# Eight pairs of heads in one pipeline per layer, with a written order for TensorE and more work for GpSimd

## The chip, the cores and the metric

The kernel runs on one core of a Trainium2 chip. A core has five engines that each work through a queue of their own in order: TensorE (PE, the matrix engine; PEld is its weight load), VectorE (DVE), ScalarE (ACT), GpSimd (POOL) and SyncE (SP), which here issues most of the transfers. They meet only at semaphores. The metric is the time of one execution on the device in microseconds. The kernel before takes 591.89 us (median of 3 runs, 590.76 to 593.34).

## What is computed

A trunk of two decoder layers on 256 tokens of width 1024, in float32. Layer 0 has two groups of heads side by side, layer 1 one group of 16 heads; each layer is followed by a SwiGLU network.

```python
proj = h @ w_in                                   # layer 0: c_q 256, c_kv 128, k_r 32, then qB, kB, vB of 512 each
qA = (rmsnorm(c_q, g_q) @ w_uq)                   # 8 latent heads, 64 plain + 32 rotary columns
kv = (rmsnorm(c_kv, g_kv) @ w_ukv)                # k_nope 64 and vA 64 for each head
oA = causal_attention([q_nope, rope(q_rope)], [k_nope, rope(k_r)], vA)
oB = dilated_attention(qB, kB, vB)                # 8 heads of 64, a bias for each head
h = h + concat(oA, oB) @ w_out
...
qkv = h @ w_qkv                                   # layer 1: 16 query heads, 2 key/value heads
s = q @ k.T * scale - slopes * dist               # a band of 128 keys, one sink for each head
o = softmax([s, sink])[..., :-1] @ v
h = h + o @ w_out
...
h = h + (silu(gate) * up) @ w_down                # behind the attention of each layer
```

## The kernel before

**Products.** Each float32 operand is split in two fp32r halves: a rounded half (`hi`, a cast on ACT) and the rest (`lo`, a difference on DVE). `mm3` (L106 to L116) then makes one product of three matmuls: hi by hi, hi by the weights' lo, lo by hi. A "job" below is one such triple with 512 columns.

**Weights.** `load` (L55) brings 128x2048 pieces into `raw` (three buffers) from SP's queue; `part_weight` (L70) casts them to `wh` on ACT (L83) and forms their rest `wl` on DVE (L84), in blocks of 128x512 (416 and 352 for uq). A `raw` buffer is free for the next load once its last `wl` is formed.

**Stages.** On the time axis of the profile: the c projection (0 to 17 us); the projections b, uq and ukv with the norms of c and the rotary terms (17 to 45); four pairs of latent heads "a" (45 to 79); four pairs of dilated heads "b" (79 to 113); the end of the output projection wo0 (113 to 121); the first SwiGLU network (121 to 302); kv and the first half of qc (302 to 328); eight pairs of grouped heads "c" in two calls of four (328 to 392); the end of wo1 (392 to 402); the second network (402 to 577); the end.

**One pair of heads** (`Pair`, L349) goes through: `turns` (transposes T of q and k into the PSUM bank `t`, copied to SBUF by DVE and ACT); `scores` (s, into the banks `s0` and `s1`); `softmax` (sn on DVE L373, the exponential e on ACT L378, its reciprocal and the normalising of e on DVE L383, one instruction of 128 and one of 256 columns for each head); `turn_p` for each of the two heads (transposes pT into the bank `p`, split by ACT and DVE, L395); `values` (o, into the bank `t` again, split into `oT` by ACT and DVE in two halves, L409). Each of the banks `t`, `s0`, `s1`, `p` is there once.

**What sets the order.** `attention` (L440) writes the pairs one after another, with jobs of a projection as fill between the steps: the rest of b beside the latent pairs, kt 0 to 3 of wo0 beside the dilated ones, the second half of qc beside the grouped pairs 0 to 3, kt 0 to 3 of wo1 beside 4 to 7. A scheduler of the compiler then orders the instructions of every engine by its own estimate, so the order on TensorE is not the written one: it can use fill up earlier. `OutProj.finish` does kt 4 to 7 of the output projection after the last pair. GpSimd does little: constants, the power in the norms (L197), rotary terms (L251 to L256, and L314 to L319 for one half) and copies of the sinks (L370).

Of the kernel before, what the change touches and what calls it, by code (L numbers as in the profile page):

```python
# [11 lines left out]
F32 = mybir.dt.float32  # L12
# [4 lines left out]
P = 128  # L17
D = 1024
KT = D // P
# [21 lines left out]
def trunk(ctx: ExitStack, tc: tile.TileContext, dr):  # L41
# [13 lines left out]
    def load(name, parts=1, between=None):  # L55
# [12 lines left out]
        st["raw"].append((raw, width, cut, u))  # L68

    def part_weight(name, between=None):  # L70

        _, n, kts = dr[name]
        st = streams[name]
        raw, width, cut, u = st["raw"].pop(0)
        per = n * kts
        for i in range(width // per):
            hi = wpool.tile([P, 1024], F32R, tag="wh", name=f"wh_{name}_{u}_{i}")
            lo = wpool.tile([P, 1024], F32R, tag="wl", name=f"wl_{name}_{u}_{i}")
            step = min(per, cut, 512 if per == 1024 else 416)
            for a in range(0, per, step):  # L80
                e = min(per, a + step)
                part = raw[:, i * per + a : i * per + e]
# [180 lines left out]
    def project(wname, base, per, groups, out, scale, name, parted=()):  # L263

        jobs = []
        for j in groups:
            hold = {}

            def job(j, q, b, hold):
                if q == 0 and b == 0:  # L270
                    hold["p"] = [acc(f"{name}{j}{i}") for i in range(2)]
                for i in range(per):
                    kt = per * q + i
                    mm3(hold["p"][b], actT(b, kt), piece(wname, base(j) + q).at(i, 0, 512), kt == 0, kt == KT - 1)
                if q == KT // per - 1 and j in parted:
# [7 lines left out]
                elif q == KT // per - 1:  # L283
                    t = big.tile([P, 512], F32, tag="big", name=f"{name}s{j}{b}")
                    nc.scalar.activation(t, hold["p"][b], AF.Copy, scale=scale[b])
                    out[j][b] = t

            for q in range(KT // per):
                for b in range(2):
                    jobs.append(lambda j=j, q=q, b=b, hold=hold: job(j, q, b, hold))  # L290
# [4 lines left out]
    for f in bjobs[:12]:  # L295
        f()
# [52 lines left out]
    class Pair:  # L349
# [12 lines left out]
        def softmax(self, name, ps, bias, sink):  # L362
# [76 lines left out]

    def attention(pairs, kt0, fill):  # L440
        n = len(pairs)
        total = len(fill)

        def run(share):

            want = total - int(round(total * min(1.0, share)))
            while len(fill) > want:
                fill.pop(0)()

        step = 1.0 / (n + 1)  # L450
        pairs[0].turns()
        for i in range(n + 1):
            t = i * step
            if i < n:
                pairs[i].scores()
            run(t + step / 4)
            if i > 0:
                pairs[i - 1].turn_p(0)
                run(t + step / 2)
                pairs[i - 1].turn_p(1)  # L460
            if i + 1 < n:
                pairs[i + 1].turns()
            run(t + 3 * step / 4)
            if i > 0:
                pairs[i - 1].values(kt0 + i - 1)
            run(t + step)


    def latent(p):
        half, store = p // 2, {}  # L470

        def turns():
            for i in range(2):
                k = 2 * (p % 2) + i
                pt = transposes([t[half][:, k, :] for t in (qA[0], qA[1], kA[0], kA[1])], f"a{p}{i}", 96)
                qk = work.tile([P, 512], F32, tag="qk", bufs=3, name=f"qk_a{p}{i}")
                nc.vector.tensor_copy(qk[:96, 0:256], pt[:96, 0:256])
                nc.scalar.copy(qk[:96, 256:512], pt[:96, 256:512])
                store[i] = qk

# [12 lines left out]

    attention([latent(p) for p in range(4)], 0, bjobs[12:])

    biases = {}
# [8 lines left out]
    def pair64(p, name, q, k, zk, v, bias0, sinks):  # L505

        store = {}

        def turns():
            pt = transposes([*q(), *(k() if k else ())], f"{name}{p}")  # L510
# [6 lines left out]
        return Pair(  # L517
            f"{name}{p}", turns, pair_scores(lambda: store["q"], zk), v, lambda i: bias_of(bias0 + 2 * p + i), 0.125,
            [None if sinks is None else sinks[:, 2 * p + i : 2 * p + i + 1] for i in range(2)])

    class OutProj:
        def __init__(self, wname, name):
            self.w, self.name, self.po, self.done = wname, name, None, 0

        def one(self, kt, b):
            if self.po is None:
                self.po = [[acc(f"{self.name}{b}{n}") for n in range(2)] for b in range(2)]
            for n in range(2):
                self.mm(kt, b, n)

        def mm(self, kt, b, n):
            w = piece(self.w, kt).at(0, n * 512, n * 512 + 512)
            mm3(self.po[b][n], oact(b, kt), w, kt == 0, kt == 7)

        def jobs(self, kts):
            return [lambda kt=kt, b=b: self.one(kt, b) for kt in kts for b in range(2)]

        def finish(self, kts, g):
            for b in range(2):
                for n in range(2):  # L540
                    for kt in kts:
                        self.mm(kt, b, n)
                    new_h(b, self.po[b][n], n, g, self.name)

# [7 lines left out]

    attention([dilated(p) for p in range(4)], 4, out0.jobs(range(4)))

# [84 lines left out]
    g = gain(0)  # L639
    out0.finish(range(4, 8), g)  # L640
    g1 = gain(1)
# [42 lines left out]
    out1.finish(range(4, 8), g)  # L684

# [120 lines left out]
```

## Time and profile before

| what | value |
|---|---|
| median of 3 runs | 591.89 us (590.76 to 593.34) |
| the profiled execution | 591.09 us, of it 589.3 us span |
| TensorE busy | 566.9 us (96%) |
| VectorE busy | 381.1 us (65%) |
| ScalarE busy | 335.7 us (57%) |
| GpSimd busy | 26.4 us (4%), 63 instructions |
| granted TensorE clock, mean | 0.990 |

The span runs from the first to the last instruction; 1.8 us of the execution lie outside it. A matmul's record is longer than the distance to the next one, since they overlap in the pipeline; so a busy TensorE may still hold short gaps, and where distances matter they are taken from start to start.

### The profile page before, as it was taken

How to read it: one execution, taken by the hardware profiler on the slowest of the kernel's cores; microseconds unless marked ns; L12 is line 12 of the kernel's file. 1: busy time of each engine (PE TensorE's matmuls, PEld its weight loads, DVE VectorE, ACT ScalarE, POOL GpSimd, SP SyncE). 2: the span in 40 equal slices, each digit the busy share in tenths (PEclk: the TensorE clock that was granted, in tenths of full speed). 3: DMA queues.
4: the chain of work that ended last, by engine and by line, in shares of the span. 5: the costliest groups of instructions: out<-in, count | busy, mean ns of one | idle time of the engine just before them, and what ended most of it. 6: DMA issues, size and time to landing. Idle time of an engine off the chain costs nothing.

```text
span 589.3 us, 7570 instructions
## 1 busy us (share of the span) xinstructions
PE 566.9 (96%) x2661; PEld 458.6 (78%) x2661; DVE 381.1 (65%) x842; ACT 335.7 (57%) x732; POOL 26.4 (4%) x63
## 2 busy tenths in 40 slices
PE   8999996999999999999999999889999999999995
PEld 5788875778888888888888766658888888888884
DVE  5589987696556655554468787877556556654524
ACT  6789766575455555543447867756555455554412
POOL 1250000010000000100000010001000000000000
PEclk9999997999999999999999999999999999999998
DMA  8967442337564554645628353026555565555301
GB/s 254 379 232 251 143 162 89 107 108 253 176 214 152 205 185 172 213 155 204 212 73 297 132 180 123 39 71 211 204 194 182 175 214 155 204 191 174 136 2 71
DMA packets 18183, 101.57 MB, mean 172 GB/s; under 512 B 2272, under 2 KB 3168, under 8 KB 7520
## 3 DMA queue, kind: packets, MB, share of 16 engines
q1 hardware_dynamic: 17712, 100.55, 49.6%
q10 hardware_dynamic: 432, 0.53, 0.2%
q8 instruction: 21, 0.34, 0.2%
q14 instruction: 18, 0.15, 0.1%
HBM read 100.02 MB, written 1.05 MB: 172 GB/s over the span
## 4 chain that ended last, share of the span: by engine, by line
PE 86%; DVE 4%; ACT 4%; DMA 2%; issue 2%; SPq 1%; POOL 1%; POOLq 0%; ACTq 0%; DVEq 0%
PE f1g L114 7%; PE f0g L116 7%; PE f0g L114 7%; PE f1g L116 7%; PE f0g L115 7%; PE f1g L115 7%; PE f0d L116 3%; PE f0d L115 3%; PE f0d L114 3%; PE f1d L116 3%; PE f1d L114 3%; PE f1d L115 3%; PE p L114 2%; PE p L115 2%; PE p L116 2%
## 5 line engine op out<-in xcount | busy, mean ns | idle before, releaser
L84 DVE TENSOR_TENSOR wl_gu<-raw_gu,wh_gu 128x512 fp32r<-128x512 f32 x176 | 115.5, 688 | 63.8 <-ACT wh_gu L83 63.3
L83 ACT CAST wh_gu<-raw_gu 128x512 fp32r<-128x512 f32 x176 | 102.2, 619 | 79.4 <-PE f0g L116 33.1
L84 DVE TENSOR_TENSOR wl_dn<-raw_dn,wh_dn 128x512 fp32r<-128x512 f32 x88 | 57.5, 689 | 54.8 <-ACT wh_dn L83 54.8
L83 ACT CAST wh_dn<-raw_dn 128x512 fp32r<-128x512 f32 x88 | 50.8, 619 | 61.6 <-PE f1d L116 23.3
L114 PE MATMUL f1g<-wh_gu,hTh_p 128*128 128x512 f32 x176 | 69.7, 396 | 0.5 <-ACT hTh_p L131 0.5
L114 PE MATMUL f0g<-wh_gu,hTh_p 128*128 128x512 f32 x176 | 69.6, 395 | 0.0
L116 PE MATMUL f0g<-wh_gu,hTl_p 128*128 128x512 f32 x176 | 68.9, 392 | 0.0
L116 PE MATMUL f1g<-wh_gu,hTl_p 128*128 128x512 f32 x176 | 68.8, 391 | 0.0
L115 PE MATMUL f0g<-wl_gu,hTh_p 128*128 128x512 f32 x176 | 68.5, 389 | 0.0
L115 PE MATMUL f1g<-wl_gu,hTh_p 128*128 128x512 f32 x176 | 68.5, 389 | 0.0
L116 PEld LDWEIGHTS f0g<-wh_gu,hTl_p 128*128 128x128 f32 x176 | 33.0, 188 | 7.4 <-DVE hTl_p L132 0.5
L116 PEld LDWEIGHTS f1g<-wh_gu,hTl_p 128*128 128x128 f32 x176 | 33.0, 188 | 7.4 <-DVE hTl_p L132 0.4
L114 PEld LDWEIGHTS f1g<-wh_gu,hTh_p 128*128 128x128 f32 x176 | 33.1, 188 | 7.1 <-ACT hTh_p L131 0.8
L114 PEld LDWEIGHTS f0g<-wh_gu,hTh_p 128*128 128x128 f32 x176 | 33.1, 188 | 6.8 <-ACT hTh_p L131 0.4
L115 PEld LDWEIGHTS f0g<-wl_gu,hTh_p 128*128 128x128 f32 x176 | 33.1, 188 | 6.6
L115 PEld LDWEIGHTS f1g<-wl_gu,hTh_p 128*128 128x128 f32 x176 | 33.1, 188 | 6.5
L114 PE MATMUL f0d<-wh_dn,f0fTh 128*128 128x512 f32 x88 | 34.5, 392 | 0.0
L114 PE MATMUL f1d<-wh_dn,f1fTh 128*128 128x512 f32 x88 | 34.3, 390 | 0.0
L116 PE MATMUL f0d<-wh_dn,f0fTl 128*128 128x512 f32 x88 | 34.3, 390 | 0.0
L116 PE MATMUL f1d<-wh_dn,f1fTl 128*128 128x512 f32 x88 | 34.2, 389 | 0.0
L115 PE MATMUL f1d<-wl_dn,f1fTh 128*128 128x512 f32 x88 | 34.2, 389 | 0.0
L115 PE MATMUL f0d<-wl_dn,f0fTh 128*128 128x512 f32 x88 | 34.2, 389 | 0.0
(298 smaller groups left out, 1098.6 us busy)
## 6 DMA issues: line engine op xcount, KB each, us to landing
raw_gu<-in_w_gu_dram SPq DMA_DIRECT2D x44, 1024.0 KB, 4.9
raw_dn<-in_w_dn_dram SPq DMA_DIRECT2D x22, 1024.0 KB, 4.9
raw_wo<-in_w_wo_dram SPq DMA_DIRECT2D x8, 1024.0 KB, 5.3
raw_b<-in_w_b_dram SPq DMA_DIRECT2D x4, 1024.0 KB, 7.0
raw_qc<-in_w_qc_dram SPq DMA_DIRECT2D x4, 1024.0 KB, 4.9
bias<-in_bias_dram SPq DMA_DIRECT2D x12, 256.0 KB, 3.3
raw_b<-in_w_b_dram SPq DMA_DIRECT2D x4, 512.0 KB, 6.4
gain<-in_gains_dram SPq DMA_DIRECT2D x4, 512.0 KB, 3.9
```

The lines of the kernel that those rows point to most:

```text
L83: nc.scalar.copy(hi[:, a:e], part)
L84: nc.vector.tensor_sub(lo[:, a:e], part, hi[:, a:e].bitcast(F32))
L114: nc.tensor.matmul(out, ah, wh, start=first, stop=False)
L115: nc.tensor.matmul(out, ah, wl, start=False, stop=False)
L116: nc.tensor.matmul(out, al, wh, start=False, stop=last)
```

## The change

Six edits, all in the kernel's text:

1. `rest` picks the engine that forms a weight's rest. For b, ukv, uq, wo0, kv, qc and wo1, two of three go to GpSimd; c and the networks' weights stay on VectorE.
2. The normalising of e goes from VectorE to GpSimd.
3. `project` makes one job for each kt instead of each two.
4. `attention` takes all eight pairs of a layer in one pipeline and writes TensorE's order down: inside `manual_schedule` the compiler's scheduler leaves TensorE's instructions in the order of the text. In the period of pair i stand: scores of i, one job, turns of i+1, turn_p(0) of i-1, one job, (a latent pair's second turns), turn_p(1) of i-1, the other jobs, values of i-1. `shares` says how many jobs each of the nine periods has.
5. turn_p of the second head uses the bank `s0` in place of `p`.
6. wo0 and wo1 give kt 0 to 5 as fill (24 jobs) and leave kt 6 and 7 to `finish`, which starts with kt 6 for two of the four blocks.

```diff
+    POOLED = {"b", "ukv", "uq", "wo0", "kv", "qc", "wo1"}
+    def rest(name):
+        if name not in POOLED:
+            return nc.vector
+        pooled[0] += 1
+        return nc.vector if pooled[0] % 3 == 0 else nc.gpsimd
...
-                nc.vector.tensor_sub(lo[:, a:e], part, hi[:, a:e].bitcast(F32))
+                rest(name).tensor_sub(lo[:, a:e], part, hi[:, a:e].bitcast(F32))
...
-                nc.vector.tensor_scalar(
+                nc.gpsimd.tensor_scalar(
                     out=e[:, x:y], in0=e[:, x:y], scalar1=rs[:, b : b + 1], scalar2=1.0, op0=ALU.mult, op1=ALU.mult
...
-            pp = att("p", f"pT_{self.name}{i}")
+            pp = att(("p", "s0")[i], f"pT_{self.name}{i}")
...
+        def other(i, part):
+            share = fill[i]
+            cuts = [round(len(share) * x) for x in (0, 0.2, 0.4, 0.6, 1)]
+            for f in share[cuts[part] : cuts[part + 1]]:
+                f()
...
+        with tc.manual_schedule(engines={mybir.EngineType.PE}):
+            for t in pairs[0].turns():
+                t()
+            for i in range(n + 1):
+                ahead = pairs[i + 1].turns() if i + 1 < n else []
+                if i < n:
+                    pairs[i].scores()
+                other(i, 0)
+                for t in ahead[:1]:
+                    t()
+                if i > 0:
+                    pairs[i - 1].turn_p(0)
+                other(i, 1)
+                for t in ahead[1:]:
+                    t()
+                if i > 0:
+                    pairs[i - 1].turn_p(1)
+                other(i, 2)
+                other(i, 3)
+                if i > 0:
+                    pairs[i - 1].values(i - 1)
...
+        def finish(self, g):
+            early = [(0, 0), (0, 1)]
+            with tc.manual_schedule(engines={mybir.EngineType.PE}):
+                for b, n in early:
+                    self.mm(6, b, n)
...
-    attention([latent(p) for p in range(4)], 0, bjobs[12:])
-    attention([dilated(p) for p in range(4)], 4, out0.jobs(range(4)))
+    attention(
+        [latent(p) for p in range(4)] + [dilated(p) for p in range(4)],
+        shares((6, 6, 6, 6, 5, 5, 5, 5, 4), bjobs[24:] + out0.jobs(range(6))))
-    out0.finish(range(4, 8), g)
+    out0.finish(g)
...
-    attention([grouped(p) for p in range(4)], 0, project("qc", lambda j: 4 * j, 2, [1], qC, rstd1, "qC"))
-    attention([grouped(p) for p in range(4, 8)], 4, out1.jobs(range(4)))
+    attention(
+        [grouped(p) for p in range(8)],
+        shares((5, 5, 6, 4, 4, 4, 4, 4, 4), project("qc", lambda j: 4 * j, 2, [1], qC, rstd1, "qC") + out1.jobs(range(6))))
```

How this moves instructions shows at three places. **GpSimd's queue at the start.** Here are its instructions behind the constants, of before; `rstd` is the reciprocal root of a norm, `kr` and `krt` are rotary terms.

```order
L197 TENSOR_TENSOR rstd_n_263<-ss_n_260,mhalf 128x1
L197 TENSOR_TENSOR rstd_c_274<-ssc_269,mhalf 128x2
L197 TENSOR_TENSOR rstd_n_304<-ss_n_301,mhalf 128x1
L197 TENSOR_TENSOR rstd_c_315<-ssc_310,mhalf 128x2
L251 TENSOR_TENSOR kr_292<-krn_282,rope 128x16
```

The same place on GpSimd after the change; `wl_b` and `wl_uq` are rests of weights.

```order
L94 TENSOR_TENSOR wl_b_0_218<-raw_b_214,wh_b_0_217 128x512 x2
L94 TENSOR_TENSOR wl_b_1_224<-raw_b_214,wh_b_1_223 128x512
L94 TENSOR_TENSOR wl_b_0_233<-raw_b_229,wh_b_0_232 128x512
L94 TENSOR_TENSOR wl_b_1_239<-raw_b_229,wh_b_1_238 128x512 x2
L207 TENSOR_TENSOR rstd_n_263<-ss_n_260,mhalf 128x1
L207 TENSOR_TENSOR rstd_c_274<-ssc_269,mhalf 128x2
L207 TENSOR_TENSOR rstd_n_304<-ss_n_301,mhalf 128x1
L207 TENSOR_TENSOR rstd_c_315<-ssc_310,mhalf 128x2
L94 TENSOR_TENSOR wl_b_0_399<-raw_b_252,wh_b_0_398 128x512
L94 TENSOR_TENSOR wl_b_1_405<-raw_b_252,wh_b_1_404 128x512
L94 TENSOR_TENSOR wl_uq_0_436<-raw_uq_254,wh_uq_0_435 128x416
L261 TENSOR_TENSOR kr_292<-krn_282,rope 128x16
```

Six rests of weights now stand ahead of the first norm, and three more between the norms and the twelve rotary terms; behind those terms follow two blocks of uq, one of ukv and two of the next b piece.

**ScalarE's queue before the first scores.** `qA_511` is the copy of q of the second 128 tokens, which the first transposes T need; casts of the b pieces stand around it. Of before:

```order
L83 CAST wh_b_1_618<-raw_b_610 128x512
L308 COPY qA_511<-pq_504 128x384
L83 CAST wh_b_1_618<-raw_b_610 128x512
L83 CAST wh_b_0_744<-raw_b_742 128x512
L308 COPY qA_528<-pq_521 128x384
```

The same place on ScalarE after the change:

```order
L93 CAST wh_b_1_620<-raw_b_612 128x512
L93 CAST wh_b_0_734<-raw_b_732 128x512
L320 COPY qA_511<-pq_504 128x384
L93 CAST wh_b_0_734<-raw_b_732 128x512
L93 CAST wh_b_1_740<-raw_b_732 128x512
L320 COPY qA_528<-pq_521 128x384
```

A cast of the next b piece (`raw_b_732`, the fifth) now stands ahead of `qA_511`, where before the first cast of that piece (`raw_b_742` there) stood behind it. Some rows on, still on ScalarE after the change:

```order
L141 CAST vAh_552<-pv_548 128x512
L503 COPY qk_a_571<-T_a_566 96x256
L93 CAST wh_b_0_844<-raw_b_842 128x512 x2
L93 CAST wh_b_1_850<-raw_b_842 128x512 x2
L503 COPY qk_a_579<-T_a_574 96x256
```

Four casts of the sixth b piece stand between the copies of the two heads' turned q and k.

**TensorE among the dilated pairs.** `T_b` are transposes of q and k, `pT_b` those of e, `o_b` the values, `p` the output projection. Of before, from the second dilated pair to the third:

```order
L393 MATMUL pT_b_1110<-ident,e_b_1015 128x128
L421 MATMUL T_b_1116<-ident,bs_386 128x128
L421 MATMUL T_b_1116<-ident,bs_394 128x128
L421 MATMUL T_b_1116<-ident,bs_688 128x128
L421 MATMUL T_b_1116<-ident,bs_704 128x128
L393 MATMUL pT_b_1188<-ident,e_b_1079 128x128 x3
L393 MATMUL pT_b_1194<-ident,e_b_1091 128x128 x3
L431 MATMUL s_b_1146<-kz0h,qT_b_1121 128x256
```

The same place on TensorE after the change, behind the scores of the third pair:

```order
L124 MATMUL p_1004<-wh_wo_1_0_1144,oT_a_963 128x512
L125 MATMUL p_1004<-wl_wo_1_0_1145,oT_a_963 128x512
L126 MATMUL p_1004<-wh_wo_1_0_1144,oT_a_963 128x512
L433 MATMUL T_b_1211<-ident,bs_386 128x128
L433 MATMUL T_b_1211<-ident,bs_394 128x128
L433 MATMUL T_b_1211<-ident,bs_660 128x128
L433 MATMUL T_b_1211<-ident,bs_714 128x128
L405 MATMUL pT_b_1225<-ident,e_b_1084 128x128 x3
L124 MATMUL p_1005<-wh_wo_1_0_1144,oT_a_963 128x512
L125 MATMUL p_1005<-wl_wo_1_0_1145,oT_a_963 128x512
L126 MATMUL p_1005<-wh_wo_1_0_1144,oT_a_963 128x512
L405 MATMUL pT_b_1234<-ident,e_b_1096 128x128 x3
```

Before, nothing of the projection stood between the transposes; now a job stands ahead of T and between the two pT, and three more behind them.

## Rows read from the trace of the kernel before

**Rows 1.** The page: each engine's busy time, share of the span, instructions

```profile
PE 566.9 (96%) x2661; PEld 458.6 (78%) x2661; DVE 381.1 (65%) x842; ACT 335.7 (57%) x732; POOL 26.4 (4%) x63
```

**Rows 2.** Windows: length, busy PE, PEld, DVE, ACT, POOL, clock, DMA share, GB/s

```profile
45.00:121.00 76.00, 70.80 (x364) 55.91 (x362) 64.67 (x204) 53.84 (x152) 0.80 (x2) 0.96 0.42 144
90.00:102.00 12.00, 7.46 (x29) 5.49 (x28) 8.23 (x32) 6.39 (x23) 0.00 (x0) 0.72 0.30 109
121.00:302.00 181.00, 180.96 (x823) 149.31 (x822) 105.61 (x173) 91.80 (x169) 3.30 (x5) 1.00 0.55 189
328.00:402.00 74.00, 67.14 (x334) 50.23 (x333) 60.53 (x191) 50.19 (x140) 5.68 (x15) 1.00 0.31 108
```

**Rows 3.** Waits of TensorE: waiter, releaser; us in total, times, longest

```profile
PE pT_b L393 <- DVE pTl_b L132: 3.9, 2, 2.7
PE p L114 <- ACT oT_c L131: 3.6, 2, 1.8
```

**Rows 4.** Timeline of TensorE: start, us, what; two full-rate matmuls, then the dilated pairs

```profile
46.67 0.40 PE L114 MATMUL b<-wh_b,xTh 128*128 128x512 f32 x1
46.90 0.39 PE L115 MATMUL b<-wl_b,xTh 128*128 128x512 f32 x1
...
90.33 0.60 PE L421 MATMUL T_b<-ident,bs 128*128 128x128 f32 x4
93.61 0.90 PE L393 MATMUL pT_b<-ident,e_b 128*128 128x128 f32 x3 [2.69 <-DVE pTl_b L132]
```

**Rows 5.** Timeline of all engines in the head: start, us, what

```profile
15.17 5.36 DVE L84 TENSOR_TENSOR wl_b<-raw_b,wh_b 128x512 fp32r<-128x512 f32 x8 [0.37 <-ACT wh_b L83]
...
21.29 0.56 POOL L197 TENSOR_TENSOR rstd_n<-ss_n,mhalf 128x1 f32<-128x1 f32 x1 [18.13 <-DVE ss_n L196]
...
27.61 0.70 POOL L197 TENSOR_TENSOR rstd_c<-ssc,mhalf 128x2 f32<-128x2 f32 x1 [1.62 <-DVE ssc L196]
...
32.34 3.44 SPq L65 DMA_DIRECT2D raw_b<-in_w_b_dram  x3
...
36.39 0.33 PE L115 MATMUL pq<-wl_uq,cTh 128*128 128x384 f32 x1
...
37.48 0.40 PE L115 MATMUL pk<-wl_ukv,cTh 128*128 128x512 f32 x1
...
37.83 0.62 ACT L83 CAST wh_b<-raw_b 128x512 fp32r<-128x512 f32 x1
...
40.51 0.48 ACT L308 COPY qA<-pq 128x384 f32<-128x384 f32 x1
```

**Rows 6.** GpSimd by form: busy us, mean ns; then one of its timeline rows

```profile
L251 POOL TENSOR_TENSOR kr<-krn,rope 128x16 f32<-128x16 f32 x2 | 0.4, 223 | 0.8 <-ACT krn L239 0.8
L316 POOL TENSOR_TENSOR qA<-qA,rope 128x64 f32<-128x64 f32 x2 | 0.6, 322 | 0.0
L340 POOL MEMSET kz0h<- 128x512 f32 x1 | 0.5, 526 | 0.0
...
30.61 0.67 POOL L253 TENSOR_TENSOR krt<-krn,rope 128x16 f32<-128x16 f32 x1
```

**Rows 7.** The tile raw_b: its transfers from issue to landing

```profile
DMA to landing us min/median/max: 4.8/6.4/10.0
```

**Rows 8.** Timeline of ScalarE and VectorE in the latent stage: the split of oT

```profile
60.35 0.37 ACT L131 CAST oT_a<-o_a 64x256 fp32r<-64x256 f32 x1
61.20 0.37 ACT L131 CAST oT_a<-o_a 64x256 fp32r<-64x256 f32 x1 [0.48 <-DVE oT_a L132]
...
61.67 0.43 DVE L132 TENSOR_TENSOR oT_a<-o_a,oT_a 64x256 fp32r<-64x256 f32 x1
```

**Rows 9.** VectorE by form from 45 to 121 us: busy us, mean ns

```profile
L84 DVE TENSOR_TENSOR wl_wo<-raw_wo,wh_wo 128x512 fp32r<-128x512 f32 x16 | 10.6, 681 | 0.1
...
L383 DVE TENSOR_SCALAR e_b<-e_b,rs_b 128x256 f32<-128x256 f32 x8 | 2.8, 349 | 0.0
...
L383 DVE TENSOR_SCALAR e_b<-e_b,rs_b 128x128 f32<-128x128 f32 x8 | 2.3, 283 | 0.2
```

More of the change, by code (lines that the diff above doesn't have):

```diff
@@ L68, in load @@
         st["raw"].append((raw, width, cut, u))
+    POOLED = {"b", "ukv", "uq", "wo0", "kv", "qc", "wo1"}
+    pooled = [0]
+    def rest(name):
[3 more added lines that the diff above has]
+        return nc.vector if pooled[0] % 3 == 0 else nc.gpsimd
     def part_weight(name, between=None):
@@ L267, in project, with job @@
             hold = {}
-            def job(j, q, b, hold):
-                if q == 0 and b == 0:
+            def job(j, kt, b, hold):
+                if kt == 0 and b == 0:
                     hold["p"] = [acc(f"{name}{j}{i}") for i in range(2)]
[L272 to L275, printed above, removed]
+                w = piece(wname, base(j) + kt // per).at(kt % per, 0, 512)
+                mm3(hold["p"][b], actT(b, kt), w, kt == 0, kt == KT - 1)
+                if kt < KT - 1:
+                    return
+                if j in parted:
                     hi, lo = (big.tile([P, 512], F32R, tag="big", name=f"{name}{p}{j}{b}") for p in "hl")
@@ L282, in job @@
                     out[j][b] = hi, lo
-                elif q == KT // per - 1:
+                else:
                     t = big.tile([P, 512], F32, tag="big", name=f"{name}s{j}{b}")
@@ L289, in project @@
                 for b in range(2):
-                    jobs.append(lambda j=j, q=q, b=b, hold=hold: job(j, q, b, hold))
+                    for i in range(per):
+                        jobs.append(lambda j=j, kt=per * q + i, b=b, hold=hold: job(j, kt, b, hold))
         return jobs
@@ L294, in trunk @@
     bjobs = project("b", lambda j: 4 * j, 2, range(3), qkvB, rstd, "b", (2,))
-    for f in bjobs[:12]:
+    for f in bjobs[:24]:
         f()
@@ L438, in pair_scores, with attention @@
         return run
-    def attention(pairs, kt0, fill):
+    def attention(pairs, fill):
         n = len(pairs)
[L442 to L466, printed above, removed]
+        def other(i, part):
[24 more added lines that the diff above has]
+                    pairs[i - 1].values(i - 1)
@@ L469, in latent, with shares, turn @@
+    def shares(counts, jobs):
+        out, at = [], 0
+        for c in counts:
+            out.append(jobs[at : at + c])
+            at += c
+        assert at == len(jobs), (at, len(jobs))
+        return out
     def latent(p):
         half, store = p // 2, {}
-        def turns():
[L473 to L479, printed above, removed]
+        def turn(i):
+            k = 2 * (p % 2) + i
+            pt = transposes([t[half][:, k, :] for t in (qA[0], qA[1], kA[0], kA[1])], f"a{p}{i}", 96)
+            qk = work.tile([P, 512], F32, tag="qk", bufs=3, name=f"qk_a{p}{i}")
+            nc.vector.tensor_copy(qk[:96, 0:256], pt[:96, 0:256])
+            nc.scalar.copy(qk[:96, 256:512], pt[:96, 256:512])
+            store[i] = qk
+        def turns():
+            return [lambda: turn(0), lambda: turn(1)]
@@ L507, in pair64, with turn @@
         store = {}
-        def turns():
+        def turn():
             pt = transposes([*q(), *(k() if k else ())], f"{name}{p}")
@@ L517, in pair64 @@
         return Pair(
-            f"{name}{p}", turns, pair_scores(lambda: store["q"], zk), v, lambda i: bias_of(bias0 + 2 * p + i), 0.125,
+            f"{name}{p}", lambda: [turn], pair_scores(lambda: store["q"], zk), v, lambda i: bias_of(bias0 + 2 * p + i), 0.125,
             [None if sinks is None else sinks[:, 2 * p + i : 2 * p + i + 1] for i in range(2)])
@@ L523, in __init__, with mm @@
             self.w, self.name, self.po, self.done = wname, name, None, 0
-        def one(self, kt, b):
+        def mm(self, kt, b, n):
             if self.po is None:
                 self.po = [[acc(f"{self.name}{b}{n}") for n in range(2)] for b in range(2)]
-            for n in range(2):
-                self.mm(kt, b, n)
-        def mm(self, kt, b, n):
             w = piece(self.w, kt).at(0, n * 512, n * 512 + 512)
@@ L535, in jobs @@
         def jobs(self, kts):
[L536 to L543, printed above, removed]
+            return [lambda kt=kt, b=b, n=n: self.mm(kt, b, n) for kt in kts for b in range(2) for n in range(2)]
+        def finish(self, g):
[3 more added lines that the diff above has]
+                    self.mm(6, b, n)
+                for b in range(2):
+                    for n in range(2):
+                        if (b, n) not in early:
+                            self.mm(6, b, n)
+                        self.mm(7, b, n)
+                        new_h(b, self.po[b][n], n, g, self.name)
     out0 = OutProj("wo0", "p0")
@@ L679, in grouped @@
             lambda b: [vC[b][:, a + g * P : a + (g + 1) * P] for a in (0, 256)], 8, nsink)
-    attention([grouped(p) for p in range(4)], 0, project("qc", lambda j: 4 * j, 2, [1], qC, rstd1, "qC"))
-    attention([grouped(p) for p in range(4, 8)], 4, out1.jobs(range(4)))
+    attention(
+        [grouped(p) for p in range(8)],
+        shares((5, 5, 6, 4, 4, 4, 4, 4, 4), project("qc", lambda j: 4 * j, 2, [1], qC, rstd1, "qC") + out1.jobs(range(6))))
     g = gain(2)
-    out1.finish(range(4, 8), g)
+    out1.finish(g)
     gf = gain(3)
```

## The prediction

> **What bounds the kernel now.** I read the page first: TensorE is busy 96% of the span, the next engine 65% [rows 1]. So only gaps of TensorE can be won, and work taken from VectorE pays only where TensorE waits for VectorE. The windows say where the gaps are [rows 2]: the first network, 121 to 302 us, is full (180.96 of 181). From 45 to 121 us, the even attention, TensorE is busy 70.80 of 76 us; from 328 to 402, the odd one, 67.14 of 74. That understates the gaps: a record of 512 columns lasts 0.40 us, but the next matmul starts 0.23 us later [rows 4], so a gap of up to 0.17 us hides in it. Added from start to start over the 364 and 334 matmuls of the two rows, less the back-to-back distance of each shape, the excess is 11.7 us (even) and 13.1 us (odd). These 24.8 us are the ceiling of what the written order can return.
>
> The waits tell the kind [rows 3]: transposes pT wait for the split of the pT before them (3.9 us, two waits), a projection job waits for oT (3.6 us, two). The timeline shows the worst place [rows 4]: behind T at 90.33 nothing is left but the next pT, which starts at 93.61. The fill is used up there: between T and the two pT, before has no job, after has one ahead, one between and three behind (the order in the change section). In the window around it, 90 to 102 us, TensorE is busy 7.46 of 12 us and the granted clock is 0.72 [rows 2], between its two levels of 1.2 and 2.4 GHz, after it had idled 2.69 us.
>
> **Term 1, the even attention: 5.0 us won.** What stays of 11.7? The bank `t` is there once: T of pair i+1 waits until oT of pair i-2 is split. That split takes from 60.35 to 61.67 + 0.43 = 62.10, 1.75 us, in four steps that wait for each other [rows 8], and starts some 0.25 us behind the last values matmul: 2.0 us. TensorE reaches T after the scores (six matmuls, 1.03 us at the back-to-back distance; 0.66 for a latent pair) and one job (0.68): 1.71 or 1.34 us. So it waits 0.3 us, or 0.65, and some 0.3 us more for what VectorE does in between: five periods, 4 x 0.6 + 0.95 = 3.4 us. Rests of the network's weights (0.68 us each, as wl_wo [rows 9]) stay on VectorE ahead of it in later periods, 0.9 us. The start and the last period, 0.8 us; the end, where kt 7 waits for the last oT, 2.0 less two jobs and the jobs' own gaps, 1.6 us. Sum 6.7; 11.7 - 6.7 = 5.0. Bounds: 9 us if VectorE is always ready, 1 us if every period waits twice as long.
>
> **Term 2, the odd attention: 5.9 us won.** The same way: the first T has no fill ahead of it (the last qC is copied, turned and split), 1.7 us; five waits for `t` of 0.5 us, 2.5; the end 1.2; small gaps 1.8. Sum 7.2; 13.1 - 7.2 = 5.9. Bounds 2 and 9 us.
>
> **Term 3, normalising e: nothing.** It leaves VectorE (283 and 349 ns [rows 9], 64 instructions in all) for GpSimd. There no row shows it; bounds for 128 and 256 columns are the 128x16 difference (0.22 us) and that of 512 worked out below (1.2). I take 0.35 and 0.6 us, 1.9 us a pair. Its cover is the period of 5.7 to 7.3 us between the exponentials and pT; without it every period loses what is late.
>
> **Term 4, rests on GpSimd in the head: 7.5 us lost.** First the price. Two-input instructions take 0.22 us at 16 columns and 0.32 at 64 [rows 6]: 2.1 ns a column, so about 1.2 us at 512, against 0.68 on VectorE. Below stands the memset of 512 columns, 0.53 us, that reads nothing; above, the same rotary instruction beside VectorE's differences, 0.67 in place of 0.22 [rows 6], so up to 1.7. I take 1.2, being the same kind of instruction.
> The Trainium skill, "GPSIMD Engine Reference", section 3.1, gives 4497 ns for a two-input add on GpSimd against 2293 on VectorE, 1.96 times, and section 1 names contention between the two for SBUF. The contention agrees with 0.67 against 0.22; by the ratio 0.68 would become an estimated 1.33 us, and this term some 0.7 us larger. It speaks against this edit.
> Now the path. (a) GpSimd starts at 15.17, as VectorE's eight rests did [rows 5]; six of 1.2 us end at 22.4, and the first norm behind them, at 21.29 before, is 1.1 us late (0 at 0.53 us a piece, 4 at 1.7). The turned c and all behind it wait. (b) The last norm then ends at 29.4 rather than 28.3 [rows 5]; two rests of b and one of uq go to 32.8, twelve rotary terms (4.3 us in before, from 28.27 to 33.34 less a pause) to 37.1, two of uq and one of ukv to 38.0, 39.0 and 40.2. TensorE wants them at 36.39 + 1.1 and, each shifted, 0.5 us later and at pk, 37.48 + 1.1 [rows 5]: waits of 0.5, 0.5 and 0.6 us, 1.6 together. (c) The fifth b piece goes into uq's raw buffer. Before, it was one of the three transfers issued from 32.34 to 35.8 [rows 5]; now it is issued at 39.0. A lone one lands in 4.8 us [rows 7], at 43.9. ScalarE's queue has its first cast ahead of the copy qA_511: cast and copy (0.62 and 0.48 us [rows 5]) and VectorE's rotation, six instructions of 0.22 us (some 0.9), end at 45.9. TensorE comes to that transpose at 44.3: 1.6 us. (d) The second head's T waits for ScalarE to copy the first, and its own copy stands behind four casts: 0.6 + 1.3 + 1.7 = 3.6 us by the same durations. Less 0.4 us of gaps that before had there: 1.1 + 1.6 + 1.6 + 3.6 - 0.4 = 7.5 us. Bounds 2 (price 0.6, no transfer late) and 11 (1.7, or a lower clock as in the 0.72 window).
>
> **Term 5, rests of kv, qc and wo: 0.3 us lost.** Norms in the odd head stand behind one of them, up to 0.5 us; those of wo are formed a period early, hidden by the jobs before. On SP the loads of wo wait for GpSimd's rests in place of VectorE's; each has a whole period.
>
> **Edits with no term.** Bank `s0` for the second pT frees `p` earlier; jobs of one kt cost the same matmuls; fewer jobs at the end are in terms 1 and 2. None can lose, since `s0` is copied long before.
>
> **Sum.** 591.09 us (profiled) - 5.0 - 5.9 + 7.5 + 0.3 = 588.0. The profiled execution is 0.8 us under the median; against the median that is **588.8 us**, 0.5% faster, at the edge of what a measurement of this kernel can tell from no change (about 0.5%).
>
> **The rivals.**
> *The head is cheap.* If the rests cost about 0.7 us on GpSimd and the casts arrive in time, term 4 shrinks to 3 us: 588.8 - 4.5 = 584.3; with VectorE emptier, half of the waits for `t` go as well, some 3 us: about 582. For it: VectorE, busy 64.67 of 76 us in the even attention [rows 2], gives up two thirds of the 10.6 us of wl_wo and all normalising, 5.1 us for the dilated half alone [rows 9]. Against it: 0.22 to 0.32 us for 48 columns.
> *The order is not worth its waits.* If a fixed TensorE order stalls where the scheduler stepped aside, and the gains of terms 1 and 2 halve, 588.8 + 5.4 = 594.2. For it: one bank `t`; against: the gaps of [rows 3] are gaps of missing fill.
> *Slower: GpSimd becomes the bound of each period.* Beside VectorE's differences everything on GpSimd takes 0.45 us more [rows 6]: four normalisings 3.7 us, two to three rests 4.6 us; 8.3 us in a period of 5.7 to 7.3 us. Then e comes late to pT by some 1 us in ten of the 16 periods: 588.8 + 10 = about 599. It decides from the point where GpSimd's busy time passes the period. Against it: at prices without contention GpSimd needs 4.5 us.
>
> **How the numbers follow.** Forecast (584.5 to 593) 0.42; head cheap 0.27; order halved 0.11; GpSimd bound 0.20. Faster by over 0.5% is half of the forecast's case and all of the second, 0.48; within 0.5% 0.29; slower 0.23. The forecast's own range is 584.5 to 593, and it holds both signs; to hold 8 in 10 the range goes from 580 (most of the second) to 598 (nearly half of the last).
>
> **What will show it.** GpSimd's 128x512 rest: 1.2 us or not. The first rstd_n later than 21.3 us. The first latent scores: near 52 us, rather than 45.5. No gap like that of 90 us, and the clock at 1.00 there. T waiting for oT's split by 0.3 to 0.9 us in five periods of each layer. The prediction is wrong if GpSimd's instructions cost under 0.8 us, if the waits for `t` are absent or double, or if pT waits for e from GpSimd.

## The result, and the profile after

The changed kernel takes 600.21 us (median of 4 runs, 599.46 to 601.36) against 591.62 us before; the ratio is 1.0143 (95% interval 1.0114 to 1.0172). It is slower by 8.6 us, where 588.8 us was forecast and 580 to 598 allowed.

The page of the changed kernel, engines' busy time, answers to [rows 1]. TensorE's busy time is that of before (567.3 for 566.9 us), GpSimd's has gone from 26.4 to 120.4 us, VectorE's from 381.1 to 354.3: the span grew by gaps.

```profile
PE 567.3 (95%) x2661; PEld 461.5 (77%) x2661; DVE 354.3 (59%) x723; ACT 337.9 (57%) x732; POOL 120.4 (20%) x182
```

The windows of the changed kernel (columns as in [rows 2]), cut at its own stages:

```profile
0.00:40.00 40.00, 33.69 (x142) 24.84 (x143) 18.15 (x39) 25.25 (x54) 22.23 (x38) 1.00 0.70 247
40.00:57.50 17.50, 10.94 (x42) 7.69 (x40) 13.33 (x23) 10.74 (x24) 14.26 (x22) 0.83 0.65 224
57.50:131.60 74.10, 70.76 (x364) 56.93 (x364) 50.64 (x156) 53.44 (x149) 29.02 (x45) 0.97 0.40 136
131.60:312.00 180.40, 180.40 (x822) 149.14 (x821) 102.28 (x166) 90.49 (x166) 7.96 (x9) 1.00 0.56 190
312.00:337.00 25.00, 22.73 (x132) 19.20 (x131) 17.48 (x23) 16.64 (x35) 16.20 (x13) 1.00 0.52 174
337.00:405.00 68.00, 62.69 (x325) 50.22 (x324) 46.98 (x143) 50.11 (x138) 28.52 (x56) 1.00 0.35 118
```

The first network starts at 131.6 us, where it started at 121.3: more than the whole loss lies ahead of it. From there to the second network it is 273.2 us instead of 275.3, a gain of 2.1. The row from 40 to 57.5 us is the place: TensorE busy 10.94 of 17.5 us at a clock of 0.83, while GpSimd is busy 14.26. The first matmul of the first network, before and after:

```profile
121.27 0.50 PE L114 MATMUL f0g<-wh_gu,hTh_p 128*128 128x512 f32 x1
131.64 0.49 PE L124 MATMUL f0g<-wh_gu,hTh_p 128*128 128x512 f32 x1
```

The waits of TensorE in the changed kernel (columns as in [rows 3]). The waits of [rows 3] are gone; these stand in their place:

```profile
PE T_a L433 <- DVE qA L330: 5.1, 2, 2.6
PE T_c L433 <- DVE oT_c L142: 3.7, 5, 0.8
PE cT L252 <- DVE cg L244: 2.0, 2, 1.3
PE c L124 <- ACT xTh L170: 1.8, 2, 1.2
PE T_kC L433 <- DVE kz0l L142: 1.4, 1, 1.4
PE T_b L433 <- DVE oT_a L142: 1.3, 2, 0.8
```

T_c and T_b behind oT are the waits for the one bank `t` that the prediction named. The largest wait it did not name: T_a behind VectorE's rotary terms (L326 to L331). The timeline of VectorE there, in the changed kernel:

```profile
40.78 1.04 DVE L326 TENSOR_TENSOR ropet<-qA,rope 128x64 f32<-128x64 f32 x1 [2.70 <-ACT qA L320]
41.74 1.31 DVE L327 TENSOR_TENSOR ropet<-qA,rope 128x64 f32<-128x64 f32 x1
42.98 1.30 DVE L329 TENSOR_TENSOR qA<-qA,rope 128x64 f32<-128x64 f32 x1
44.20 0.36 DVE L328 TENSOR_TENSOR qA<-qA,rope 128x64 f32<-128x64 f32 x1
```

The same instructions took 0.22 us in before, and so did the copy of kr behind them. The first of each, of before:

```profile
41.41 0.22 DVE L314 TENSOR_TENSOR ropet<-qA,rope 128x64 f32<-128x64 f32 x1
37.88 0.22 DVE L329 COPY kA<-kr 128x128 f32<-128x128 f32 x1
```

In the changed kernel three of the instructions last 1.04 to 1.31 us, about as long as one of GpSimd's differences (1.29 us for 128x512), which run without a pause from 38.7 to 44.2 us, the last three of them on 128x512. And GpSimd's queue at the start (answers to the row at 21.29 in [rows 5]):

```profile
15.74 8.45 POOL L94 TENSOR_TENSOR wl_b<-raw_b,wh_b 128x512 fp32r<-128x512 f32 x6 [12.59 <-ACT wh_b L93]
24.15 0.56 POOL L207 TENSOR_TENSOR rstd_n<-ss_n,mhalf 128x1 f32<-128x1 f32 x1
```

Six rests take 8.45 us and the first norm starts at 24.15 instead of 21.29. By form, GpSimd's new instructions cost (busy us, mean ns; the clean price of a rest is 1.29 us, two of the six took 1.77 and 1.73):

```profile
L94 POOL TENSOR_TENSOR wl_b<-raw_b,wh_b 128x512 fp32r<-128x512 f32 x16 | 21.4, 1364 | 16.0 <-ACT wh_b L93 15.8
...
L395 POOL TENSOR_SCALAR e_b<-e_b,rs_b 128x256 f32<-128x256 f32 x8 | 3.8, 479 | 0.0
...
L395 POOL TENSOR_SCALAR e_b<-e_b,rs_b 128x128 f32<-128x128 f32 x8 | 3.0, 372 | 16.2 <-DVE rs_b L393 16.2
```

### The profile page after: what moved, and what is told of

Same layout as the page of the kernel before. It is cut to its first block, busy times and chain, and to the rows that moved or that the text cites. A ratio compares the mean times of both kernels' runs of the same rounds, so it can differ in the third digit from the quotient of the medians.

```text
span 597.7 us, 7692 instructions
## 1 busy us (share of the span) xinstructions
PE 567.3 (95%) x2661; PEld 461.5 (77%) x2661; DVE 354.3 (59%) x723; ACT 337.9 (57%) x732; POOL 120.4 (20%) x182
## 4 chain that ended last, share of the span: by engine, by line
PE 79%; DVE 7%; ACT 5%; DMA 3%; issue 3%; POOL 1%; SPq 0%; POOLq 0%; DVEq 0%; ACTq 0%
PE f1g L126 7%; PE f0g L126 7%; PE f1g L124 7%; PE f0g L124 7%; PE f0g L125 7%; PE f1g L125 7%; PE f0d L124 3%; PE f0d L126 3%; PE f0d L125 3%; PE f1d L126 3%; PE f1d L124 3%; PE f1d L125 3%; DMA raw_b<-in_w_b_dram 2%; PE p L124 2%; PE p L125 2%
## 5 line engine op out<-in xcount | busy, mean ns | idle before, releaser
L94 DVE TENSOR_TENSOR wl_dn<-raw_dn,wh_dn 128x512 fp32r<-128x512 f32 x88 | 57.5, 689 | 54.8 <-ACT wh_dn L93 54.7
```

What stands on the lines that cost most here:

```text
L94: rest(name).tensor_sub(lo[:, a:e], part, hi[:, a:e].bitcast(F32))
```

## The experiments

Fifteen kernels, each timed beside the kernel before on the same chip. To place a difference I read two marks in each profile: the first matmul of the first network (121.3 us before, 131.6 after) and the distance from there to the first of the second network (275.3 and 273.2). A mark is of one execution, and executions of one kernel lie 1 to 3 us apart, so a difference of marks of that size is a hint and no proof.

**The head's rests back on VectorE.**

```diff
-    POOLED = {"b", "ukv", "uq", "wo0", "kv", "qc", "wo1"}
+    POOLED = {"wo0", "kv", "qc", "wo1"}
```

> The changed kernel, but the rests of b, uq and ukv are formed on VectorE again; wo, kv and qc stay shared with GpSimd. Theory (GpSimd's queue and its meeting with VectorE cost the head some 14 us): the first latent scores come back from 56 us to within 3 us of before's 45.5, and the time falls from 600.2 to 588 to 590. Rival (the written order of TensorE, with transposes ahead of work that could run, costs the head): the stall before the first scores stays and the time stays above 596.

588.97 us, ratio to before 0.9952 (0.9933 to 0.9971), as the theory said. First scores at 47.1 us (45.5 in before, 56.0 in the changed kernel), first network at 122.1. So 11.2 us of the changed kernel are the rests of b, uq and ukv on GpSimd, and the written order, which is still there, does not make the stall: the rival falls.

**No rests on GpSimd.**

```diff
-    POOLED = {"b", "ukv", "uq", "wo0", "kv", "qc", "wo1"}
+    POOLED = set()
```

> The changed kernel with every rest on VectorE; e is still normalised on GpSimd. Theory: as in the run before this one, and the 2 to 3 us lost between the first network and the grouped pairs come back too: 585 to 588. Rival (VectorE needs the relief in the pairs): the waits for oT grow by over 3 us in each attention, and it is slower than the run that leaves only the head to VectorE.

589.62 us, 0.9956 (0.9940 to 0.9972). Not the 585 to 588 of the theory. The distance between the networks shrinks to 271.2 (the rests of kv and qc cost 2 us), as it said, but the first network starts at 124.2 instead of 122.1. The rival's sign is absent: T waits for oT 0.1 us longer in the grouped pairs and 0.6 in the dilated ones, not over 3. What this profile does show is the clock: 0.50 for 6.8 us in the latent pairs, where the kernel with the head's rests on VectorE had 1.00, behind a wait of 1.25 us and in one of 1.04 that both kernels have. So the marks do not show that the rests of wo on GpSimd had helped there.

```profile
47.80:54.60 6.80, 6.48 (x20) 5.25 (x21) 5.37 (x17) 4.04 (x13) 2.31 (x3) 0.50 0.69 254
```

**The rests alone, in the kernel before.**

```diff
-                nc.vector.tensor_sub(lo[:, a:e], part, hi[:, a:e].bitcast(F32))
+                rest(name).tensor_sub(lo[:, a:e], part, hi[:, a:e].bitcast(F32))
```

> The kernel before, with only the rests shared with GpSimd (two of three of b, uq, ukv, wo, kv, qc). Theory: the head loses on its own without any written order, 8 to 14 us, and 2 us behind the first network: 600 to 606. Rival (the loss needs TensorE's written order, and the scheduler works around late rests): 590 to 594.

608.88 us, 1.0280 (1.0258 to 1.0303): worse than any forecast of it. First network 11.9 us late, and 5.5 us more between the networks. The rival falls: without the written order the scheduler does not work around the rests, and the kernel loses more than with all six edits.

**The written order alone** (rests and normalising on VectorE).

```diff
-    POOLED = {"b", "ukv", "uq", "wo0", "kv", "qc", "wo1"}
+    POOLED = set()
...
-                nc.gpsimd.tensor_scalar(
+                nc.vector.tensor_scalar(
```

> The changed kernel with every rest and the normalising of e on VectorE: the written order of TensorE and the pipelines of eight pairs alone. Theory (the order wins what the trace shows of it, 11.7 to 8.3 us and 13.1 to 8.8 us of gaps): 582 to 586. Rival (VectorE becomes late without GpSimd, its 22 us of normalising stand ahead of oT): 588 to 593.

591.18 us, 0.9980 (0.9966 to 0.9994). The rival's number. Between the networks 271.4 us, 3.9 won; but the first network starts at 123.5, 2.2 lost. These marks flatter it: the profiled execution (589.52 us) is the fastest of its ten. Its waits of TensorE:

```profile
PE T_c L433 <- DVE oT_c L142: 3.2, 5, 0.7
PE T_a L433 <- ACT qk_a L503: 2.3, 3, 1.3
PE T_b L433 <- DVE oT_a L142: 1.6, 2, 1.1
...
PE o_b L416 <- DVE kz0l L142: 1.1, 1, 1.1
PE s_a L514 <- ACT qk_a L503: 1.0, 1, 1.0
PE o_a L416 <- DVE kz1l L142: 0.9, 1, 0.9
```

T_a and s_a behind qk_a are 2.3 us at the start of the pipeline, where no job stands between the first transposes, and 1.0 us in the next two periods. In before the scheduler had put work there: by the windows up to the first scores (45.54 us in before, 45.73 here) TensorE does 187 matmuls in before and 177 here, and the ten are done later.

```profile
0.00:45.54 45.54, 41.84 (x187) 32.46 (x188) 30.52 (x77) 33.56 (x73) 14.55 (x39) 1.00 0.80 287
0.00:45.73 45.73, 40.28 (x177) 30.80 (x178) 30.56 (x76) 33.51 (x73) 14.38 (x39) 1.00 0.80 283
```

The rival's reason holds for the values behind kz, not for oT: with the normalising on GpSimd and all rests on VectorE (the run two above) the waits for kz are 0.8 us instead of 2.6, and T's for oT are no shorter.

**The rotary products read q from PSUM** (changed kernel otherwise).

```diff
+            pr = r if half else pq[:, :384].rearrange("p (h f) -> p h f", f=96)
+            y1, y2 = pr[:, :, 64:80], pr[:, :, 80:96]
-            eng.tensor_mul(tt[0], x2, nsin)
+            eng.tensor_mul(tt[0], y2, nsin)
...
```

> The changed kernel with one thing altered: VectorE's four rotary products (L326 to L329) read q from PSUM instead of from its copy in SBUF, so that they have one SBUF input instead of two; the two sums behind them keep two. Theory (VectorE's instructions with two SBUF inputs wait for a whole rest of GpSimd: 1.0 to 1.3 us instead of 0.22 in the changed kernel): the four take 0.2 to 0.4 us each, the first transpose T_a comes 2 us earlier, and the same for the second block; 600.2 less 3 to 5 us. Rival (it is only the late copy of q behind casts that wait for the b piece): the products stay at 1.0 to 1.3 us or the waits before T_a stay 2.6 us each, time 599 to 601.

598.37 us, 1.0103 (1.0084 to 1.0121). The first scores come at 53.7 instead of 56.0 us. The timeline of VectorE in this kernel, at the place shown above:

```profile
40.26 0.22 DVE L328 TENSOR_TENSOR ropet<-pq,rope 128x64 f32<-128x64 f32 x1 [2.47 <-ACT qA L320]
40.40 0.22 DVE L329 TENSOR_TENSOR ropet<-pq,rope 128x64 f32<-128x64 f32 x1
40.53 0.21 DVE L330 TENSOR_TENSOR qA<-pq,rope 128x64 f32<-128x64 f32 x1
40.66 0.21 DVE L331 TENSOR_TENSOR qA<-pq,rope 128x64 f32<-128x64 f32 x1
40.79 0.56 DVE L332 TENSOR_TENSOR qA<-qA,ropet 128x64 f32<-128x64 f32 x1
41.27 1.33 DVE L333 TENSOR_TENSOR qA<-qA,ropet 128x64 f32<-128x64 f32 x1
42.53 1.32 DVE L343 COPY kA<-kr 128x128 f32<-128x128 f32 x1
```

And GpSimd's beside them:

```profile
39.99 1.28 POOL L94 TENSOR_TENSOR wl_ukv<-raw_ukv,wh_ukv 128x512 fp32r<-128x512 f32 x1
41.22 2.54 POOL L94 TENSOR_TENSOR wl_b<-raw_b,wh_b 128x512 fp32r<-128x512 f32 x2
```

This is the cause in one picture. While GpSimd forms wl_ukv (39.99 to 41.27), the four products with one operand in PSUM take 0.22 us; the first sum with both operands in SBUF, begun at 40.79, ends when that rest ends, and the next lasts through GpSimd's next. The copy of kr, SBUF to SBUF with one operand, waits the same way (1.32 us). The gain in time is only 1.8 us, under the forecast 3 to 5: the sums and copies still wait, and of the 2.4 us won at the first scores 0.8 are left at the first network of the two profiles.

**T into bank p, the first pT into bank t** (on the kernel with the head's rests on VectorE).

```diff
-            pp = att(("p", "s0")[i], f"pT_{self.name}{i}")
+            pp = att(("t", "s0")[i], f"pT_{self.name}{i}")
...
-        pt = att("t", f"T_{name}")
+        pt = att("p", f"T_{name}")
```

> The kernel with the head's rests on VectorE (589.0 us), with two PSUM banks exchanged: the transposes T go to bank p and the first head's pT to bank t, so T no longer waits for oT of two pairs before. Theory (the one bank t costs the written order 0.5 to 1 us in most periods, 7 us over both attentions): the waits of T for oT vanish, 582 to 585. Rival (what frees bank t late only moves to pT or to the values): 587 to 590.

590.20 us, 0.9970 (0.9959 to 0.9982), against 588.97 without the exchange: the theory falls. The wait has only moved, as this kernel's waits say:

```profile
PE pT_c L405 <- DVE oT_c L142: 3.4, 6, 0.8
```

TensorE waits for oT as long as before, now with the pT that took bank t.

**Normalising alone on GpSimd, in the kernel before.**

```diff
-                nc.vector.tensor_scalar(
+                nc.gpsimd.tensor_scalar(
```

> The kernel before, with only the normalising of e on GpSimd. Theory (371 and 479 ns in place of 283 and 349; it empties VectorE by 22 us and reads one SBUF operand): within 2 us of before, the better for it where pT waited for VectorE, 589 to 592. Rival (it comes later to pT in a queue that waits for the exponentials, and pT waits for it): 593 to 597.

592.32 us, 1.0011 (0.9996 to 1.0025): no change, near the theory's 589 to 592. But the wait that the rival named is in the trace, and other stages make up for it: the first network starts 2.4 us later, and the distance between the networks is 1.4 us shorter.

```profile
PE pT_a L393 <- POOL e_a L383: 2.1, 1, 2.1
...
PE pT_b L393 <- POOL e_b L383: 0.9, 2, 0.6
```

**Of the head only b shared.**

```diff
-    POOLED = {"b", "ukv", "uq", "wo0", "kv", "qc", "wo1"}
+    POOLED = {"b", "wo0", "kv", "qc", "wo1"}
```

> The changed kernel, but uq and ukv form all rests on VectorE; b still shares them with GpSimd. Theory: the raw buffers of uq and ukv come free some 4 us earlier, so the fifth and sixth b pieces land before ScalarE's queue needs them, and the half of the loss that hangs on them returns: 594 to 597. Rival (the b rests ahead of the norms and beside VectorE's rotary instructions make nearly all of it): 598 to 600.

597.89 us, 1.0102 (1.0076 to 1.0127). Uq and ukv are worth 2.3 us of the 11.2, b's rests 8.9: nearer to the rival than to the theory of late raw buffers, and the 2.3 us are no more than the two intervals together.

**Of b only the first two pieces, or only the later four** (uq and ukv on VectorE).

```diff
-    POOLED = {"b", "ukv", "uq", "wo0", "kv", "qc", "wo1"}
+    POOLED = {"b", "wo0", "kv", "qc", "wo1"}
...
-                rest(name).tensor_sub(lo[:, a:e], part, hi[:, a:e].bitcast(F32))
+                (rest(name) if name != "b" or u < 2 else nc.vector).tensor_sub(lo[:, a:e], part, hi[:, a:e].bitcast(F32))
```

and, for the later pieces, `u >= 2` in place of `u < 2`.

> Of the head's rests only those of the first two b pieces are shared with GpSimd, the six that stand ahead of the first norm; wo, kv and qc as in the changed kernel. Between 589.0 us (no b rest on GpSimd) and 597.9 us (all). Theory (the queue ahead of the norms costs 2 to 3 us, the first norm starts at 24.2 instead of 21.3 us; the rest of the loss is VectorE waiting for GpSimd later): 591 to 592.5. Rival (late norms make most of it): 595 to 598.

> The complement: of the head's rests only those of the third to sixth b piece are shared with GpSimd. Theory (VectorE's rotary instructions and copies take 1.0 to 1.3 us beside GpSimd's rests, twice six of them on the way to the transposes T_a): 594 to 596. Rival: under 592.

592.43 us, 1.0005 (0.9988 to 1.0022), and 596.02 us, 1.0068 (1.0048 to 1.0088). Both as the theory said. Against 588.97 the first pieces cost 3.5 us and the later ones 7.0. The two do not add up to the 8.9 of all six, and they are not quite clean: every third rest is counted through the program, so with fewer rests of b others of wo, kv and qc go to GpSimd (20 of 32 of wo with the first pieces, 22 otherwise). With the first pieces alone VectorE's rotary terms are back at 0.22 us and the first norm starts at 25.21; with the later ones alone nothing stands ahead of the norm, and the rotation of the second 128 tokens waits: TensorE stands 3.8 us for it. A row of VectorE's timeline, first of the kernel with the first pieces shared:

```profile
45.34 0.22 DVE L326 TENSOR_TENSOR ropet<-qA,rope 128x64 f32<-128x64 f32 x1
```

and of the kernel with the later pieces shared:

```profile
42.54 1.35 DVE L326 TENSOR_TENSOR ropet<-qA,rope 128x64 f32<-128x64 f32 x1 [0.25 <-ACT qA L320]
```

**Rests of wo alone on GpSimd.**

```diff
-    POOLED = {"b", "ukv", "uq", "wo0", "kv", "qc", "wo1"}
+    POOLED = {"wo0", "wo1"}
```

> The changed kernel with rests on GpSimd for wo0 and wo1 alone; nothing moved at the start. Against the run that shares wo, kv and qc (589.0 us) it tells what the rests of kv and qc cost: theory 2 to 2.5 us (the gaps of 1.0 and 1.5 us before the grouped pairs vanish), 586 to 587; rival (they are hidden): 588.5 to 589.5.

586.84 us, 0.9922 (0.9905 to 0.9938): kv and qc cost 2.1 us, as the theory said, and the rests of wo on GpSimd win 2.8 us against none (589.62). By what wait they win is not shown.

**Two jobs at the start of each pipeline**, on top of that.

```diff
-            for t in pairs[0].turns():
+            first = pairs[0].turns()
+            if len(first) == 1:
+                fill[0].pop(0)()
+            for t in first:
                 t()
+                fill[0].pop(0)()
```

> The changed kernel with rests on GpSimd for wo0 and wo1 alone, and two jobs of each pipeline's first period moved ahead of its first scores, one beside each of the first transposes. Theory (the written order loses its gain in the even half because its pipeline starts without fill: gaps of 1.4, 1.2 and 1.0 us around the first transposes and scores): these gaps shrink by 2 to 3 us in the even and 1 us in the odd half against the same kernel without the jobs: 582 to 585. Rival (the fill taken there is missing from the first period, where the exponentials come late): the same time as the run without the jobs, within 1 us.

584.98 us, 0.9890 (0.9875 to 0.9905): 1.9 us less than without. That is inside the 582 to 585 of the theory, but less than the 3 to 4 us that it added up.

**Casts of oT and kz ahead of their rests**, on top of that.

```diff
...
-                split(po[rows, 256 * i : 256 * i + 256], o[rows, 0:256], o[rows, 256:512])
+                nc.scalar.copy(o[rows, 0:256], po[rows, 256 * i : 256 * i + 256])
+            for i in range(2):
+                rows = slice(64 * i, 64 * i + 64)
+                nc.vector.tensor_sub(
+                    o[rows, 256:512], po[rows, 256 * i : 256 * i + 256], o[rows, 0:256].bitcast(F32))
```

The split of kz is changed in the same way.

> As the run with fill at the start, and the two halves of oT (and of kz) are cast one after the other before their rests are formed, so ScalarE's second cast no longer waits for VectorE's first rest. Theory (T waits for oT's split, a chain of four steps that takes 1.75 us of which 0.48 is this wait): each of T's ten waits shrinks by 0.3 to 0.5 us, and those of the values for kz too: 3 to 5 us less, 578 to 581. Rival (VectorE's queue decides, its other work stands ahead of the rests): under 1 us less.

581.50 us, 0.9836 (0.9821 to 0.9851), 3.5 us less again and the best of all kernels here. ScalarE's second cast had waited for VectorE's first rest of the same tile [rows 8]; now both casts follow each other. T's waits for oT shrink from 3.8 and 1.4 us (T_c and T_b in the run before this one) to:

```profile
PE T_b L439 <- DVE oT_a L426: 0.6, 1, 0.6
PE T_c L439 <- DVE oT_c L426: 0.5, 2, 0.3
```

T_a's wait for qk_a grew from 1.4 to 2.3 us at the same time.

**The same casts in the kernel before.**

> The kernel before, with only the casts of oT's and kz's halves ahead of their rests. Theory (in before the gaps are gaps of missing fill, in which oT's split is the chain that TensorE waits for): 1 to 3 us less, 589 to 591. Rival: no change, 591.5 to 592.5.

590.29 us, 0.9978 (0.9964 to 0.9992): 1.5 us, as the theory said and less than under the written order, where T waits for oT's split.

**The best kernel with every rest and the normalising on VectorE.**

> The best kernel so far (581.5 us: fill at the start, untied splits) with all rests and the normalising of e back on VectorE. Theory (in the pairs VectorE's queue stands ahead of oT's split, and GpSimd takes 22 us of normalising and 16 us of rests off it): 584 to 588. Rival (the order and the untied split are the whole gain): 581 to 582.5.

586.88 us, 0.9915 (0.9897 to 0.9932), as the theory said. So 5.4 us of the best kernel are GpSimd's, with normalising and the rests of wo only. The theory's place is not the one the waits show. T's waits for oT stay small (0.7 us for T_b, none listed for T_c). VectorE's queue stands ahead of the rests of kz and pT that the values need:

```profile
PE o_c L418 <- DVE pTl_c L142: 1.1, 4, 0.4
PE o_b L418 <- DVE kz1l L361: 1.1, 1, 1.1
PE o_b L418 <- DVE kz0l L361: 1.1, 1, 1.1
```

In the best kernel o_b waits 0.2 us for each kz, and o_c's wait is not in the list.

## Why the prediction was wrong

The sign was wrong, 588.8 for 600.2, a miss of 11.4 us. About half is gain that did not come: terms 1 to 3 were to win 10.9 us, and the order, the normalising and the rests of wo won 5.3 together. The head cost 3.7 us more than summed, kv and qc 1.8.

**Term 4, the head: 7.5 forecast, 11.2 measured, and one step of it false.** The price was right: 1.29 us a rest where 1.2 was taken from two short instructions. Step (a), the late norm, was half of the truth: 1.1 us forecast, 24.15 - 21.29 = 2.9 us in the trace, since the first rest starts at 15.74 instead of 15.17 and two of the six met VectorE's and took 1.7 us. Step (b) said 1.6 us; the trace lists 0.4 for pk and nothing for pq. Step (c) failed. It took VectorE's rotation at "six instructions of 0.22 us (some 0.9)" and let the late fifth piece hold ScalarE's copy. In the trace the fifth piece, issued at 40.5 us, landed 4.9 us later, and ScalarE cast it after 47.4 us with no wait for the transfer. (A transfer held a copy at another place: the fourth piece's cast waited 2.44 us for it, and the first copy of q, behind that cast, ran at 40.27, some 0.8 us after its product.) TensorE waited twice, 2.6 and 2.5 us, for the rotation: the first one lasted from 40.78 to 45.11 us, 4.3 instead of 0.9. I had read contention in [rows 6] in one direction only, as a price on GpSimd's instructions, and carried the rows of VectorE over unchanged; and that the engines "meet only at semaphores" does not hold for these two. Reading one operand from PSUM brought the products back to 0.22 us, which shows the cause; with the later b pieces alone, 7.0 us slower, TensorE waited 3.8 us for the rotation. Step (d), 3.6 us, was smaller in the changed kernel (T_a 0.9 us behind qk_a).

The clock adds to it. In the first wait for T_a the granted clock fell to 0.50, its lower level of 1.2 GHz, from 44.8 to 48.2 us, and it was 0.50 again from 55.0 to 61.8, after the second wait and one more of 0.9 us:

```profile
44.80:48.20 3.40, 3.03 (x9) 2.74 (x10) 2.27 (x6) 1.27 (x3) 1.15 (x5) 0.50 0.88 351
55.00:61.80 6.80, 6.66 (x21) 5.20 (x22) 4.17 (x15) 5.49 (x17) 4.77 (x6) 0.50 0.74 240
```

These 10.2 us at half the clock hold some 5 us less of TensorE's work, an estimate from the two rows. Before had 0.50 from 93.3 to 100.1 us, from its wait of 2.69 on, a fall that the changed kernel lacks; the kernel with the head's rests on VectorE had 1.00 in all three places. The bound of 11 us named a lower clock, the taken value did not.

**Term 1, the even order: 5.0 forecast, nothing measured.** With the order alone the first network starts 2.2 us late. The waits for `t` were there, in number and size near the forecast. The step that failed is the list of what stays: the start without fill stood in it at 0.8 us together with the last period, and T_a and s_a wait 3.3 us behind qk_a (two jobs there won 1.9 us over both pipelines); the values behind kz did not stand in it, and wait 2.6 us.

**Term 2, the odd order: 5.9 forecast, 3.9 read from the profile of the order alone.** Right in kind; T waited for oT 3.2 us where 2.5 was summed.

**Term 3, normalising: zero forecast, and zero in the kernel before (0.6 us, inside the interval).** Under the written order it won 1.6 us (591.18 to 589.62), little more than the two intervals. Its durations, 0.37 and 0.48 us, lay near the taken 0.35 and 0.6. In the changed kernel's listed waits no pT waits for it; in the kernel before, without the order, pT waited 3.0 us for it, and that the time stayed the same there is a balance of two stages.

**Term 5: 0.3 us lost forecast.** It was two larger numbers that nearly cancel: kv and qc lose 2.1 us, wo wins 2.8. The sum's reason, norms behind a rest on GpSimd, is not in the trace: GpSimd stood idle for 5.26 and 1.29 us ahead of the two norms there. It is the contention of the head again, as in this product of VectorE's, 0.68 us in before:

```profile
320.98 1.78 DVE L595 TENSOR_TENSOR hg_f<-h,gain 128x512 f32<-128x512 f32 x1
```

T_kC waits 1.4 us there, a wait that the kernel with the rests of wo alone does not list.

As steps from one kernel to the next the parts are: order -0.9, normalising -1.6, wo -2.8, kv and qc +2.1, head +11.2, together +8.0 of 8.6 us. Such steps end at the changed kernel by construction, so their sum proves none of them; each is the difference of two medians, and the three first ones are not far from the intervals.

**The rivals.** The one on the slower side gave about 599 us, near the number, by another mechanism: GpSimd as the bound of each period. It is not that: GpSimd is busy 29.0 of 74.1 us in the even pairs and 28.5 of 68 in the odd ones. That the head is cheap was wrong. That the order's gains fall short was right in kind and too mild: alone it won 0.9 of 10.9 us, where the rival halved them.

## What to carry to other kernels

Work that goes from VectorE to GpSimd must be priced on VectorE's remaining instructions too: list what VectorE runs at that time, which of these have all operands in SBUF, and let each wait for one whole instruction of GpSimd. Keep the moved work where VectorE reads PSUM or where nobody waits for VectorE, and off a queue that carries a norm. Before a written order is judged, list what each engine hands to TensorE in one period, the start included; untying ScalarE's second cast from VectorE's first rest was worth 3.5 us, more than the order alone (0.9).

## What the runs showed of the hardware that I had not expected

VectorE's short instruction waits for GpSimd's long one: 0.22 us became 1.04 to 1.35 us beside a difference of 1.29 us, for two SBUF operands and also for a plain SBUF copy (1.32 us). With one operand in PSUM it took 0.22 us beside the same difference. The waiting goes both ways: where both engines formed rests of 512 columns at once, from 15.7 to 24.2 us, two of GpSimd's took 1.77 and 1.73 us instead of 1.29, and one of VectorE's 1.46 instead of 0.69. GpSimd's instruction with one tensor operand (normalising) took 0.37 and 0.48 us in all three kinds of pairs. The Trainium skill, "GPSIMD Engine Reference", section 1, names contention with VectorE's instructions that have two SBUF inputs; these rows agree and give its size. Section 3.1 of that page of the Trainium skill gives a ratio of 1.96 between the two engines for a two-input add; here it is 1.29 to 0.68 us, 1.9.
